# A log-sum-exp kernel with VectorE's instruction stream aligned to a block of 128

## The chip, the cores and the metric

The kernel runs on one core of a Trainium2 chip. A core has five engines with an instruction stream each: TensorE (PE in the profile), VectorE (DVE), ScalarE (ACT), GpSimd (POOL) and SyncE (SP). Here SyncE issues all the transfers, which sixteen DMA engines carry out. The metric is device time in microseconds, the median of several runs. The profile shows one execution; its span runs from the kernel's first instruction to its last.

## The reference

For each row of `x`, 32 x 512 rows of 1024 numbers in fp32, the logarithm of the sum of exponentials is computed, with the row's maximum taken out for safety.

```python
def reference(x):                      # x: 32 x 512 x 1024, standard normal
    max_x = np.max(x, axis=-1, keepdims=True)
    return (max_x.squeeze(-1) + np.log(np.sum(np.exp(x - max_x), axis=-1))).astype(np.float32)
```

## The kernel before

The 16,384 rows are spread over 128 partitions, 128 rows for each: 112 in one part, and the last 16 from another region of the input. The kernel sums the exponentials without the maximum, and checks afterwards that all sums are finite and of sane size. Only if they aren't does a fallback block repeat the work with the maximum (`with nc.If(all_fine < 1)`); on this data it is jumped over.

The rows come in through 18 loads of falling size (`LOADS`, from 16 rows for each partition to three quarters of a row) into a buffer `ring` that holds 48 rows for each partition. SyncE issues them (L130). The first load is moved ahead of the opening barrier. The next two wait for nothing but that barrier; from the fourth on, SyncE waits until the rows that lay in that part of the ring have been summed.

ScalarE takes the exponential of each load in place (L209). The sums are shared out by the letters in `LOADS`: for `R` VectorE reduces whole rows (L220); for `G` GpSimd first adds the two halves of each row (L215) and VectorE reduces the result (L146); for `T`, at the end, VectorE adds halves and accumulates in one instruction (L154). The very last quarters of a row are accumulated by ScalarE itself (L204). ScalarE then takes logarithms, and SyncE stores the results in two parts (L241 and, last of all, L251).

The order of the work on each engine is the order of the calls in the program: there is no scheduler. Waits on counted semaphores are written out by the small class `Counted`.

The closing part matters here. VectorE checks the sums (L161, L165), TensorE adds up the findings over the partitions (L171, L172, L255), and VectorE turns the number into a flag `fine` (L259). ScalarE and VectorE each load the flag into a register (L262) and branch (L311). On good sums both jump over their part of the fallback, which on VectorE is eleven instructions. Behind the jump each of the two signals SyncE (the signal of VectorE is L312, that of ScalarE is also shown under L311). SyncE waits for both signals, clears the semaphores (L315) and then waits for the last store (L317), with which the kernel ends.

The opening part is a barrier over all five engines, in three rounds (L355 and L59). VectorE's body, its first reduction, comes behind it.

Of the kernel before, what the change touches and what calls it, by code (L numbers as in the profile page):

```python
# [49 lines left out]
def kernel(  # L50
# [5 lines left out]
    nc = tc.nc  # L56
# [59 lines left out]
    stored = nc.alloc_semaphore("stored")  # L116

    nc.scalar.preload_act_table_set("natural_log_exp_and_others")  # L118
    pool.did(nc.gpsimd.memset(ones, 1.0))  # L119
    constants = pool.did(nc.gpsimd.memset(far, 100 * HIGH))  # L120

# [249 lines left out]
```

## Time and profile before

| What | us |
|---|---|
| median of 3 runs (162.53 to 162.91) | 162.78 |
| the profiled execution's own time | 162.55 |
| its span | 161.2 |
| VectorE busy | 119.1 |
| ScalarE busy | 115.1 |
| GpSimd busy | 32.4 |
| data read and written | 67.18 MB, 417 GB/s over the span |

A row of a line's view gives the engine, the operation, how often it ran, the shortest, middle and longest duration in nanoseconds, and the first and the last start in microseconds. An engine's name with a small q (DVEq, ACTq, SPq) stands for its sequencer: branches, semaphore steps and DMA issues, which don't count as busy. A row of the waits reads: who waited, for whom, microseconds in total, how often, the longest. The DMA view lists the packets by queue: their number, megabytes, and the time that they took as a share of sixteen engines over the window asked for. Times are counted from the start of the span, and a window may begin before it or end behind it.

### The profile page before, as it was taken

Reading aid. Unit: us, or ns where it says so; the run is one execution under the profiler, and the core shown is the slowest. Engines: PE = TensorE matmul, PEld = TensorE weight load, DVE = VectorE, ACT = ScalarE, POOL = GpSimd, SP = SyncE. Lnnn points to the kernel's source line nnn. Section 1 sums busy time; section 2 is a strip of 40 time slices with the busy share of each in tenths; the row PEclk is TensorE's granted clock in tenths of the full one; section 3 lists DMA queues with packets and bytes.
Section 4 is the critical chain, followed back from the end, with each engine's and each line's share of the span. In section 5 each row is a group of like instructions: output and inputs, shape, how many; then the busy total and the mean of one; then the engine's idle time right before and its main releaser. Section 6 shows DMA issues by size and latency. Waiting matters only on the chain.

```text
span 161.2 us, 183 instructions
## 1 busy us (share of the span) xinstructions
PE 0.5 (0%) x10; PEld 0.3 (0%) x10; DVE 119.1 (74%) x48; ACT 115.1 (71%) x32; POOL 32.4 (20%) x15
## 2 busy tenths in 40 slices
PE   0000000000000000000000000000000000000000
PEld 0000000000000000000000000000000000000000
DVE  0000000019999499995999999999999999999995
ACT  3000059980799609994199928996997999799995
POOL 0000000000000000000008800007950806727600
DMA  7996996996996996997999989898998999999990
GB/s 276 504 520 276 504 520 276 504 520 293 488 520 293 488 520 293 488 520 325 429 469 469 469 376 424 377 483 385 454 454 384 419 439 411 409 429 414 424 407 12
DMA packets 2880, 67.18 MB, mean 417 GB/s; under 512 B 576, under 2 KB 576, under 8 KB 1344
## 3 DMA queue, kind: packets, MB, share of 16 engines
q1 hardware_dynamic: 2880, 67.18, 97.2%
HBM read 67.11 MB, written 0.07 MB: 417 GB/s over the span
## 4 chain that ended last, share of the span: by engine, by line
DVE 53%; DMA 30%; ACT 12%; POOL 4%; PE 0%; issue 0%
DVE sumexp L220 38%; DMA ring<-in_x_dram 30%; ACT ring L209 12%; DVE sumexp L146 10%; POOL ring L215 4%; DVE ring L154 4%; DVE clamped L161 1%; DVE total L165 0%; PE count L171 0%; DVE fine L259 0%; PE count L255 0%; PE count L172 0%
## 5 line engine op out<-in xcount | busy, mean ns | idle before, releaser
L209 ACT ACTIVATE ring<-ring 128x16384 f32<-128x16384 f32 (+22 forms) x26 | 112.4, 4371 | 42.7 <-DMA ring<-in_x_dram 42.6
L220 DVE TENSOR_REDUCE sumexp<-ring 128x16 f32<-128x16384 f32 (+6 forms) x10 | 96.1, 9639 | 40.0 <-ACT ring L209 40.0
L215 POOL TENSOR_TENSOR ring<-ring 128x1024 f32<-128x1024 f32 (+5 forms) x9 | 32.1, 3573 | 118.3 <-ACT ring L209 118.3
L146 DVE TENSOR_REDUCE sumexp<-ring 128x2 f32<-128x1024 f32 (+5 forms) x9 | 16.1, 1802 | 0.4 <-POOL ring L215 0.4
L154 DVE SCALAR_TENSOR_TENSOR ring<-ring 128x512 f32<-128x512 f32 (+1 forms) x11 | 6.5, 642 | 0.0
L118 ACT ACT_TABLE_LOAD x1 | 1.3, 1283 | 1.4 <-PEq L59 1.4
L161 DVE SCALAR_TENSOR_TENSOR clamped<-sumexp 128x114 f32<-128x114 f32 (+1 forms) x2 | 0.9, 472 | 0.1
L204 ACT ACTIVATE ring<-ring 128x768 f32<-128x768 f32 x1 | 0.8, 843 | 0.1
L171 PE MATMUL count<-far,bad 128*1 128x1 f32 x4 | 0.4, 163 | 159.1 <-DVE total L165 159.1
L154 DVE DVE_READ_ACCUMULATOR ring<-ring 128x1 f32 x11 | 0.8, 76 | 0.0
L171 PEld LDWEIGHTS count<-far,bad 128*1 128x1 f32 x4 | 0.2, 80 | 159.2 <-POOL ring L215 151.1
L259 DVE TENSOR_SCALAR fine<-count 1x1 int32<-1x1 f32 x1 | 0.1, 146 | 0.4 <-PE count L255 0.4
L165 DVE TENSOR_REDUCE total<-sumexp 128x1 f32<-128x114 f32 (+1 forms) x2 | 0.4, 210 | 0.0
L172 PE MATMUL count<-total,ones 128*1 128x1 f32 x4 | 0.4, 163 | 0.0
L245 ACT ACTIVATE res<-sumexp 128x15 f32<-128x15 f32 x1 | 0.2, 215 | 0.1
L119 POOL MEMSET ones<- 128x1 f32 x1 | 0.1, 98 | 1.0 <-POOLq L59 1.0
L195 ACT ACTIVATE res<-sumexp 128x112 f32<-128x112 f32 x1 | 0.3, 280 | 0.0
L247 ACT ACTIVATE res<-sumexp 128x1 f32<-128x1 f32 x1 | 0.3, 278 | 0.0
L172 PEld LDWEIGHTS count<-total,ones 128*1 128x1 f32 x4 | 0.2, 81 | 0.0
L255 PE MATMUL count<-sumexp,ones 128*1 128x1 f32 x2 | 0.2, 163 | 0.0
L204 ACT ACTIVATION_READ_ACCUMULATOR ring<-ring 128x1 f32 x1 | 0.2, 187 | 0.0
L161 DVE DVE_READ_ACCUMULATOR clamped<-sumexp 128x1 f32 x2 | 0.2, 79 | 0.0
(6 smaller groups left out, 0.6 us busy)
## 6 DMA issues: line engine op xcount, KB each, us to landing
ring<-in_x_dram SPq DMA_DIRECT2D x1, 7376.0 KB, 24.9
ring<-in_x_dram SPq DMA_DIRECT2D x1, 5936.0 KB, 19.6
ring<-in_x_dram SPq DMA_DIRECT2D x1, 4768.0 KB, 16.4
ring<-in_x_dram SPq DMA_DIRECT2D x1, 3520.0 KB, 15.2
ring<-in_x_dram SPq DMA_DIRECT2D x1, 2976.0 KB, 21.9
ring<-in_x_dram SPq DMA_DIRECT2D x1, 1792.0 KB, 27.6
ring<-in_x_dram SPq DMA_DIRECT2D x1, 1520.0 KB, 25.2
ring<-in_x_dram SPq DMA_DIRECT2D x1, 1360.0 KB, 19.5
```

The costliest lines, as they stand in the source:

```text
L118: nc.scalar.preload_act_table_set("natural_log_exp_and_others")
L146: at = dve.did(nc.vector.reduce_sum(out=sumexp[:, c0 : c0 + s], in_=half, axis=AX.X))
L154: return dve.did(nc.vector.scalar_tensor_tensor(out=lo, in0=lo, scalar=1.0, in1=v[:, h : 2 * h], op0=ALU.mult, op1=ALU.add, accum_out=sume ...
L161: dve.did(nc.vector.scalar_tensor_tensor(out=clamped[:, c0:c1], in0=sumexp[:, c0:c1], scalar=LOW, in1=sumexp[:, c0:c1], op0=ALU.max, op1=A ...
L165: at = dve.did(nc.vector.reduce_sum(out=total[:, k : k + 1], in_=sumexp[:, c0:c1], axis=AX.X))
L171: pe.did(nc.tensor.matmul(count, lhsT=bad[:, k : k + 1], rhs=far, start=k == 0, stop=False))
L172: pe.did(nc.tensor.matmul(count, lhsT=ones, rhs=total[:, k : k + 1], start=False, stop=False))
L195: ln_early = act.did(nc.scalar.activation(out=res[:, 0:W], in_=sumexp[:, 0:W], func=AF.Ln))
L204: last = act.did(nc.scalar.activation(out=v, in_=v, func=AF.Exp, accum_out=sumexp[:, NC : NC + 1]))
L209: at = act.did(nc.scalar.activation(out=v, in_=v, func=AF.Exp))
L215: folded.append((c, p, s, pool.did(nc.gpsimd.tensor_tensor(out=rows[:, :, 0:H], in0=rows[:, :, 0:H], in1=rows[:, :, H:d], op=ALU.add,))))
L220: users.append((p, p + s * d, dve, dve.did(nc.vector.reduce_sum(out=sumexp[:, c : c + s], in_=rows, axis=AX.X))))
```

## The change

One line is added ahead of the kernel's first work instructions:

```diff
     nc.scalar.preload_act_table_set("natural_log_exp_and_others")
+    nc.vector.addr_align(128)
     pool.did(nc.gpsimd.memset(ones, 1.0))
     constants = pool.did(nc.gpsimd.memset(far, 100 * HIGH))
```

It is a directive in VectorE's stream. [...] The directive asks that the instruction that follows it on VectorE be placed at a multiple of 128 instructions; the space up to there is filled with instructions that do nothing, up to 127 of them. On VectorE it stands behind the last round of the opening barrier and ahead of the first reduction (L220). No work instruction, wait or transfer is added, removed or put into another order on any engine, and the streams of the other four engines stay as they were. All lines behind it have a number higher by one in the changed kernel.

## The prediction

> **What bounds the kernel.** I read the page first, then the chain of work that ended last, then the waits, and last the closing instructions line by line. The page's first part:
>
> ```profile
> span 161.2 us, 183 instructions
> PE 0.5 (0%) x10; PEld 0.3 (0%) x10; DVE 119.1 (74%) x48; ACT 115.1 (71%) x32; POOL 32.4 (20%) x15
> ```
>
> VectorE (DVE) has the longest list of work instructions, 48, and is busy for 74% of the span. The chain, in order of time (start, length, what), shows where that matters:
>
> ```profile
> 0.00 21.80 DMA ring<-in_x_dram
> ...
> 52.96 26.86 DMA ring<-in_x_dram
> ...
> 79.85 5.33 ACT ring L209
> ...
> 85.25 6.72 POOL ring L215
> ...
> 92.00 3.35 DVE sumexp L146
> 95.35 20.39 DVE sumexp L220 x2
> ...
> 159.71 0.15 DVE fine L259
> ```
>
> Up to 79.8 us the transfers set the time. From 92.00 on the chain is VectorE almost without a break, until the last small result `fine` at 159.86. The waits say when VectorE starts at all, and who closes the program:
>
> ```profile
> DVE sumexp L220 <- ACT ring L209: 40.0, 3, 35.7
> ...
> SPq L315 <- DVEq L312: 1.2, 1, 1.2
> ```
>
> VectorE's first reduction waits until 35.7 us. At the end the queue of SyncE (SP) waits for VectorE's closing signal, L312. This change touches only where instructions lie, so what follows `fine` is the place to look. The rows of lines L262, L311, L312, L315 and L317, each from the view of that line (duration, then start):
>
> ```profile
> L262 DVEq TENSOR_LOAD <-fine x1: 544/544/544, 159.9 to 159.9; - x1
> L311 ACTq COMPARE_BRANCH  x1: 45/45/45, 160.4 to 160.4; - x1
> L311 DVEq COMPARE_BRANCH  x1: 67/67/67, 160.5 to 160.5; - x1
> L311 ACTq EVENT_SEMAPHORE  x1: 17/17/17, 160.5 to 160.5; - x1
> L312 DVEq EVENT_SEMAPHORE  x1: 21/21/21, 161.0 to 161.0; - x1
> L315 SPq EVENT_SEMAPHORE_RANGE_CLEAR  x1: 71/71/71, 161.1 to 161.1; - x1
> L317 SPq EVENT_SEMAPHORE  x1: 17/17/17, 161.2 to 161.2; - x1
> ```
>
> The printed starts are coarse, so I asked the same views for windows of 0.01 us. ScalarE's (ACT's) branch is in progress in 160.42 to 160.43 and not in the next one, and its signal starts in 160.54 to 160.55: it needs 0.11 us from branch to signal. VectorE's branch ends in 160.54 to 160.55, and its signal starts only in 161.03 to 161.04: 0.49 us for the same step, a taken jump over the fallback block. Nothing in the profile is awaited there. SyncE's clear (L315) starts in 161.07 to 161.08, and L317 in 161.19 to 161.20, 0.12 us later; the span ends with it.
>
> **The change, part by part.**
>
> *The padding.* The directive stands behind the opening barrier (L59) and ahead of VectorE's first reduction. To reach a multiple of 128 takes at most 127 filler instructions on VectorE. The nearest rows for one filler are VectorE's four opening barrier steps:
>
> ```profile
> L59 DVEq DRAIN  x2: 10/10/10, 0.8 to 1.2; - x2
> L59 DVEq EVENT_SEMAPHORE  x2: 21/21/21, 1.1 to 1.4; - x2
> ```
>
> One lasts at least 0.01 us, so the least is 127 x 0.01 = 1.3 us. Four of them, waits included, fill 0.8 to 1.4 us, 0.15 each, so the most is 127 x 0.15 = 19 us. Both ends lie in the idle time from 1.4 to 35.7, 34.3 us. I take zero. Without that cover every microsecond of filler would lengthen the chain by one. Nothing else queues behind the filler: VectorE owes nobody anything before its first reduction ends, and SyncE's loads two and three do not wait for it.
>
> *The instruction blocks.* The trace has a queue for instruction fetches. Its answers for three windows, in this order: the microsecond from -9 to -8, the whole kernel up to 161.6, and 161.63 to 161.64:
>
> ```profile
> q14 instruction: 4, 0.03, 8.6%
> ...
> q1 hardware_dynamic: 2880, 67.18, 97.0%
> ...
> GB/s 0 0 0 0 0 0 0 0 0 0 0 0 0 0 0 0 0 0 0 0 0 0 0 0 0 0 0 0 32768 0 0 0 0 0 0 0 0 0 0 0
> q14 instruction: 1, 0.01, 332.5%
> ```
>
> Four blocks are fetched before the kernel starts. None is fetched while it runs: the second window has only the data queue. One more starts at 161.637 (the 29th fortieth of that window), behind the end of the span. A fortieth of 0.01 us at 32768 GB/s is 8192 bytes, and the first window's 0.03 MB for four agrees: a fetch is 8 KB. Alone, one takes 0.086 x 16 engines x 1 us / 4 = 0.34 us; the late one takes 3.325 x 16 x 0.01 = 0.53 us.
>
> So exactly one engine comes to a new block in this run, right about the end. VectorE has the longest stream, and it is the engine with the odd 0.49 us at its branch. I read the two together: VectorE's block boundary lies between its branch and the target, and the jump over it costs the excess. This is an inference; the trace doesn't name the engine that the fetch serves. With the body at the start of a block, the 48 work instructions, the loads of `fine`, the branch and the eleven fallback instructions behind it fit into 128, and branch and target share a block.
>
> *What it saves.* VectorE's own factor over ScalarE on the branch is 67/45 = 1.5, so without a boundary I expect 0.11 x 1.5 = 0.17 us for its exit, and the signal 0.49 - 0.17 = 0.32 us earlier, at 160.71. SyncE's clear would follow at 160.76 and L317 could run from 160.88. But L317 waits for the last store:
>
> ```profile
> 159.50 0.34 SPq L251 DMA_DIRECT2D out_dram<-res  x1
> ...
> DMA to landing us min/median/max: 1.4/1.4/1.4
> ```
>
> It lands at 159.50 + 1.4 = 160.9. With about 0.03 to 0.04 for the release (161.04 to 161.075 in the step from signal to clear), L317 starts at 160.94 in place of 161.19. The store is what is late next, and 0.25 us is what remains of 0.32. If the exit falls only to 0.35, the saving is 0.49 - 0.35 = 0.14, not yet limited by the store; if the store lands 0.07 earlier, it is 0.32. If the gap is simply VectorE's way to branch, it is zero.
>
> [...]
>
> *What it moves.* If entering a block sets off the fetch of the following one, the fetch now at 161.637 goes to the first microseconds, into the loads:
>
> ```profile
> 0.00:20.00 20.00, 0.00 (x0) 0.00 (x0) 0.00 (x0) 1.28 (x1) 0.34 (x6) 1.00 1.00 419
> ```
>
> The last two columns are the DMA engines' busy share, 1.00, and 419 GB/s: no room is left there. One 8 KB packet holds one of sixteen engines for 0.34 us. Shared by all it would be 0.02 us; if just that engine brings the last part of the load that lands at 79.8, the chain is late by the whole 0.34; if it isn't the last, by nothing. I take 0.02, which rounds away, since a load waits for one engine in sixteen, and keep 0.34 for the range. A fetch that VectorE has to wait for at the start is covered like the filler: even queued behind the whole first load it is there by 21.8 us, ahead of 35.7.
>
> **The sum.** The profiled execution took 162.55 us, its span 161.2 and 1.35 around it. Padding 0, exit -0.25, fetch +0.02 and so nothing: -0.25, a span of 160.95 and 162.30 for that execution. The median of the runs shown is 162.78, 0.23 above it, so I forecast 162.78 - 0.25 = 162.53 us, 0.15% less. About 0.2%, 0.33 us, is what a measurement of this kernel can tell from no change: the three runs shown spread over 0.38.
>
> **The rivals.**
>
> *The exit keeps its 0.49 us* because this is how VectorE leaves a branch, or because the late fetch belongs to another engine. [...] Against it: ScalarE's 0.11, and VectorE's branch itself is only 1.5 times as long. Time 162.78.
>
> *The fetch collides with the loads: slower.* Place: one DMA engine in the first 79.8 us. It decides when that engine is the last of the sixteen in the fourth load, and the exit gains nothing. Time 162.78 + 0.34 = 163.12. For it: the DMA share of 1.00. Against it: it must be the wrong engine, and the exit's saving, if it comes, pays for 0.25 of it, which leaves 162.87, inside 0.2%.
>
> *More than the exit is freed.* The late fetch, 161.64 to 162.17, lies inside the 1.35 us around the span. If VectorE's closing work waits for it, the alignment takes up to 0.53 more: 162.53 - 0.53 = 162.00, or, with half of it hidden, 162.27. For it: the fetch ends only 0.38 before the profiled execution's 162.55, if that time starts with the span. [...]
>
> **How the numbers follow.** The forecast, with the exit shorter by 0.14 to 0.32, gets 0.55; the unchanged exit 0.15; the collision 0.17; more than the exit 0.13. The forecast's saving ends just short of 0.33, and a median of few runs may fall 0.1 lower, so 0.17 of its 0.55 goes to faster and 0.38 to same. Faster: 0.17 + 0.13 = 0.30. Same: 0.38 + 0.15 = 0.53. Slower: 0.17. The range goes from 162.10, between the two ends of the third rival, to 163.10, just short of the full collision. The forecast's own range is 162.35 to 162.75.
>
> **What would show it.** Right: VectorE's signal within 0.2 us of its branch's end; L317 starting on the store's landing, near 160.9; no instruction fetch behind the span, and one in the first twenty microseconds; VectorE's first reduction still at 35.7; the fourth load landing at 79.8. Wrong: the exit still 0.49, or a fetch still at 161.6 (then it wasn't VectorE's, or the boundary isn't what costs); a first reduction later than 35.7 (the cover fails); a fourth load 0.1 or more later (the collision); or a span shorter by 0.25 with a time that doesn't follow it.

## The result

The changed kernel takes 162.96 us in the median (14 runs, 162.84 to 163.20), the kernel before 162.64 (14 runs, 162.47 to 162.97): a ratio of 1.0019, 95% interval 1.0013 to 1.0026. It is 0.3 us slower, clearly outside its own uncertainty, though just inside the 0.2% that the prediction took as the limit. The forecast was 0.25 us faster. The profiled execution took 163.01 us with a span of 161.7, against 162.55 and 161.2.

The page of the changed kernel, its first part and the DMA queues:

```profile
span 161.7 us, 240 instructions
PE 0.5 (0%) x10; PEld 0.4 (0%) x10; DVE 119.1 (74%) x48; ACT 115.0 (71%) x32; POOL 32.4 (20%) x15
...
q1 hardware_dynamic: 2880, 67.18, 97.0%
q14 instruction: 1, 0.01, 0.0%
```

The work is the same. The 57 instructions more (240 in place of 183) are the fillers, and an instruction fetch is now inside the span. Its chain of work, in order of time:

```profile
0.00 22.50 DMA ring<-in_x_dram
...
36.41 17.23 DVE sumexp L221
53.65 0.02 issue
53.66 26.90 DMA ring<-in_x_dram
...
80.58 5.33 ACT ring L210
...
92.74 3.35 DVE sumexp L147
...
160.44 0.15 DVE fine L260
```

The first load lands at 22.50 in place of 21.80. Everything behind it keeps that distance: VectorE's first reduction 36.41 (35.71), the fourth load 80.56 (79.83), VectorE's unbroken stretch from 92.74 (92.00), `fine` at 160.44 (159.71), 0.73 late. The loss is in the first load already. The rows by line:

```profile
L119 DVEq NOP  x57: 18/18/18, 1.5 to 4.1; - x57
L312 DVEq COMPARE_BRANCH  x1: 72/72/72, 161.2 to 161.2; - x1
L313 DVEq EVENT_SEMAPHORE  x1: 21/21/21, 161.4 to 161.4; - x1
L316 SPq EVENT_SEMAPHORE_RANGE_CLEAR  x1: 78/78/78, 161.5 to 161.5; - x1
L318 SPq EVENT_SEMAPHORE  x1: 17/17/17, 161.7 to 161.7; - x1
```

In windows of 0.01 us, VectorE's branch ends in 161.27 to 161.28 and its signal starts in 161.40 to 161.41: the exit fell from 0.49 us to 0.14. L318 starts in 161.65 to 161.66, so from the start of `fine` to L318 it is 1.21 us, against 161.19 - 159.71 = 1.48 before: 0.27 saved, on a chain that reaches this point 0.73 late. That makes 0.46, and the span is 161.7 against 161.2.

The fetch, asked for in the window 9.10 to 9.11 (a fortieth is 0.25 ns; the packet starts in the 21st, at 9.105):

```profile
GB/s 0 0 0 0 0 0 0 0 0 0 0 0 0 0 0 0 0 0 0 0 32768 0 0 0 0 0 0 0 0 0 0 0 0 0 0 0 0 0 0 0
q14 instruction: 1, 0.01, 193.1%
```

Its packet takes 1.931 x 16 x 0.01 = 0.31 us. Behind the span there is none any more: the window from 161.7 to 164 holds no packet at all.

### The profile page after: what moved, and what is told of

It is laid out like the page before. It is cut to its first block, busy times and chain, and to the rows that moved or that the text cites. A ratio compares the mean times of both kernels' runs of the same rounds, so it can differ in the third digit from the quotient of the medians.

```text
span 161.7 us, 240 instructions
## 1 busy us (share of the span) xinstructions
PE 0.5 (0%) x10; PEld 0.4 (0%) x10; DVE 119.1 (74%) x48; ACT 115.0 (71%) x32; POOL 32.4 (20%) x15
## 4 chain that ended last, share of the span: by engine, by line
DVE 52%; DMA 31%; ACT 12%; POOL 4%; PE 0%; issue 0%
DVE sumexp L221 38%; DMA ring<-in_x_dram 31%; ACT ring L210 12%; DVE sumexp L147 10%; POOL ring L216 4%; DVE ring L155 4%; DVE clamped L162 1%; DVE total L166 0%; PE count L172 0%; DVE fine L260 0%; PE count L256 0%; PE count L173 0%
```

## The experiments

All are the kernel before with the edit shown, next to `nc.vector.addr_align(128)`'s place in the changed kernel unless the edit says otherwise. Since the changed kernel has 57 fillers, the body of the kernel before starts at place 128 - 57 = 71 of its block. The theory after the result, from the two traces: entering a block sets off a fetch (at 9.105 in place of 161.637); a fetch among the loads makes them late (the first by 0.70); and an exit whose branch and target lie in one block is 0.35 us shorter (0.14 in place of 0.49). The traces give a fetch's size, 8 KB (32768 GB/s over 0.25 ns), and not what it brings: that it is a further block is the author's supposition.

**The fetch without the exit's saving (align_no_exit).**

```diff
+    nc.vector.addr_align(128)
+    nc.vector.addr_align(128, offset=71)
```

> The directive as in the changed kernel, and behind it a second one to place 71, so VectorE comes to a new block ahead of its body (57 fillers), and then 71 more fillers put the body back to the place in the block that it has in the kernel before. This takes the exit's saving out and leaves the fetch. Theory: fetch at 9.1 us, first load at 22.5 and fourth at 80.5 as in the changed kernel, exit 0.49, and a time 0.25 us above the changed kernel: some 0.55 to 0.7 over the kernel before, ratio 1.0035 to 1.0045. Rival (the exit's saving is worth nothing, since the store's landing or the closing sequence takes it): as the changed kernel, ratio 1.002 to 1.0025.

163.19 us against 162.60: 1.0038 (1.0024 to 1.0051), 0.6 slower. Its chain, its fillers and its closing rows:

```profile
0.00 22.39 DMA ring<-in_x_dram
...
160.34 0.14 DVE fine L261
```

```profile
L119 DVEq NOP  x57: 18/18/18, 1.5 to 4.1; - x57
L120 DVEq NOP  x71: 18/18/18, 4.6 to 7.9; - x71
L313 DVEq COMPARE_BRANCH  x1: 72/72/72, 161.1 to 161.1; - x1
L314 DVEq EVENT_SEMAPHORE  x1: 21/21/21, 161.7 to 161.7; - x1
```

The late load is there (22.39), and the exit is back at 0.50 us, since VectorE's body has its old place in a block again. A fetch behind the branch is back with it, at 162.26. The time is 0.23 us above the changed kernel's median, and by the two ratios 0.19%, 0.3 us. So the exit's saving is real and worth what the prediction said, and it is hidden under a fetch that costs twice as much. The theory's numbers held; the rival's 1.0020 to 1.0025 did not.

The fillers also show the boundary by itself. Fillers follow each other every 0.047 us (57 from 1.5 to 4.1), but between the 57th, which starts in 4.10 to 4.15, and the next, in 4.55 to 4.60, lie 0.46. So in this run VectorE's sequencer stands still for about 0.4 us (0.46 less 0.047) at the boundary, without a jump too.

**Twice the fetch (two_fetches), and an inadvertent repeat (two_blocks).**

```diff
+    nc.vector.addr_align(128)
+    nc.vector.addr_align(128, offset=1)
+    nc.vector.addr_align(128)
```

> Three directives (to 0, to 1, to 0 again): 57 + 1 + 127 fillers, two boundaries ahead of the body. In the run two_blocks the idle instruction between had been dropped, and the trace had 57 fillers. Theory: a second fetch in the first 30 us over the same DMA engine, the first or second load late by another 0.7 (23.2 in all), time 0.8 to 1.1 over the kernel before. Rival (a fetch costs the loads only once, for example as a slot that stays reserved): as the changed kernel.

163.90 us against 162.60: 1.0082 (1.0068 to 1.0096), 1.3 slower. Its DMA view for 9 to 10 and for 14 to 15 us, and its chain:

```profile
q14 instruction: 1, 0.01, 1.9%
...
q14 instruction: 1, 0.01, 2.0%
```

```profile
0.00 23.38 DMA ring<-in_x_dram
...
161.33 0.15 DVE fine L262
```

Two fetches, and the first load 1.58 later than before, 0.88 more than with one. Here each of the two fetches had its cost.

two_blocks was meant as this experiment, with an idle instruction between two directives:

```diff
+    nc.vector.addr_align(128)
+    nc.vector.nop(nofuse=True)
+    nc.vector.addr_align(128)
```

> The directive stands twice, with one idle instruction between, so VectorE comes to two new blocks ahead of its body: 57 + 1 + 127 = 185 fillers, some 9 us of 0.047, still covered by the wait to 35.7. Theory: two fetches in the first 20 us, and if both go over the same DMA engine the first load is late by up to 1.4 us, and the time 1.0 to 1.2 us over the kernel before; if a fetch costs the load only once, as the changed kernel. Exit 0.14. Rival (fillers): late by 185/57 of 0.7, 2.3 us.

The idle instruction does not appear in the trace, which has 57 fillers and one fetch, so this is the changed kernel over again. It gave 1.0029 (1.0018 to 1.0041) and a first load at 22.53, which tells only that the result repeats.

**Where the fetch falls (off127, off108, off84).**

```diff
+    nc.vector.addr_align(128, offset=127)
```

> The body begins at the last place of a block, 127: 56 fillers, one fewer than the changed kernel, but the boundary lies behind the first reduction, so the fetch starts only when VectorE goes on to the second, after 36 us. Theory: exit 0.14; the first load lands at 21.8 as before, and the load in flight at the fetch (the second, third or fourth) is the first that comes late, by about 0.7; time as the changed kernel, 0.3 us over the kernel before. Rival (fillers): the first load is late by 0.7 already, as in the changed kernel. Second rival (the first loads are late or not from one execution to the next): no tie between the fetch and the first late load.

163.04 us, 1.0027 (1.0016 to 1.0037), the exit 0.14. The first load was late at once, 22.50, as the rival had it. But the fetch was early too: it starts in the first ten microseconds, at 9.096, though VectorE's only instruction ahead of the boundary is the first reduction, which waits until 36.4. So this run does not tell fillers from fetch. It shows one fetch, at 9.096, set off while VectorE still waited on the near side.

```diff
+    nc.vector.addr_align(128, offset=108)
```

> The body begins at place 108 of a block in place of 0. The changed kernel has 57 fillers, so the body of the kernel before begins at place 71; here there are 37 fillers and the boundary lies behind the 20th work instruction, which starts at about 151 us. Theory (the lateness of the loads comes from the instruction fetch, the short exit from branch and target in one block): VectorE's exit 0.14 us as in the changed kernel; first load landed at 21.8 and fourth at 79.8 as before; one fetch at 151 to 157; time 0.25 us under the kernel before (ratio 0.9985). Rival (the fillers themselves, or the directive, make the loads late): first load later by 37/57 of 0.7, 0.45 us, and time 0.2 us over the kernel before.

163.15 us, 1.0037 (1.0024 to 1.0049). The fetch came in 96 to 97, not at 151. Its DMA view for that microsecond, its chain and VectorE's timeline:

```profile
q14 instruction: 1, 0.01, 1.9%
```

```profile
1.44 39.72 DMA ring<-in_x_dram
...
72.32 25.67 DMA ring<-in_x_dram
97.99 0.02 issue
```

```profile
116.34 2.82 DVE L147 TENSOR_REDUCE sumexp<-ring 128x5 f32<-128x2560 f32 x1 [0.56 <-POOL ring L216]
```

This is the clearest of the three. 37 fillers ran at the start, and the first loads came as before: the second landed at 41.16, where ScalarE had taken that load up at 41.15 in the kernel before. The fifth, in flight at the fetch, landed at 97.99, where ScalarE had taken it up at 97.25 before; from then on the chain is late, and VectorE, without a gap there before, waits 0.56 at 115.8. That excludes the fillers, and ties the lateness to the fetch. The gain expected did not come, because the fetch was not where I had put it.

```diff
+    nc.vector.addr_align(128, offset=84)
```

> The body begins at place 84: 13 fillers, the boundary behind the 44th work instruction, at about 159 us, still ahead of VectorE's branch. Theory: exit 0.14, first load at 21.8, one fetch behind 160; time 0.25 us under the kernel before, unless the fetch meets the last store, which would cost up to 0.3. Rival (fillers): first load later by 13/57 of 0.7, 0.16 us, time about 0.1 under the kernel before.

162.60 us, 1.0002 (0.9994 to 1.0011). The exit is 0.14, the first load lands at 21.84, but the fetch came in 155 to 156 and met the last two loads. ScalarE's and VectorE's timelines:

```profile
157.63 0.84 ACT L210 ACTIVATE ring<-ring 128x768 f32<-128x768 f32 x1 [0.74 <-DMA ring<-in_x_dram]
```

```profile
158.50 0.69 DVE L155 SCALAR_TENSOR_TENSOR ring<-ring 128x512 f32<-128x512 f32 x1 [0.27 <-ACT ring L210]
```

ScalarE waits 0.74 us for a load, which it did not before, and 0.27 of it reaches VectorE: about what the exit saves.

**The fetches of other engines (gpsimd_align, scalar_align).**

```diff
+    nc.gpsimd.addr_align(128)
```

> VectorE is left as before; the directive stands on GpSimd, ahead of its two small fills, whose results are needed only at 151 us. Theory: GpSimd comes to a new block, one fetch goes out in the first 15 us, and one DMA engine is late by about 0.7: first load landed at 22.5, VectorE's exit still 0.49, time 0.5 to 0.7 us over the kernel before (ratio 1.003 to 1.004), more than the changed kernel because nothing is saved at the exit. If the fetches of GpSimd run over another DMA engine, the load may be late by less, 0.1 to 0.7. Rival (what makes the loads late is something of VectorE): loads at 21.8, ratio 1.000.

162.94 us against 162.56: 1.0024 (1.0015 to 1.0033). GpSimd's 54 fillers ran from 1.4 to 3.5, and a fetch went out at 8.95.

```diff
+    nc.scalar.addr_align(128)
```

> VectorE is left as before; the directive stands on ScalarE, behind the request for its table and ahead of its first exponential, which waits for the first load until 21.8. Theory: as for GpSimd, one fetch in the first 15 us, first load late by up to 0.7, VectorE's exit 0.49, ScalarE's exit 0.11 as before, time 0.3 to 0.7 us over the kernel before. Rival (VectorE alone): ratio 1.000.

162.95 us, 1.0025 (1.0015 to 1.0034), 56 fillers on ScalarE, a fetch at 9.02. The chains of gpsimd_align and of scalar_align:

```profile
0.00 22.01 DMA ring<-in_x_dram
...
53.17 26.91 DMA ring<-in_x_dram
```

```profile
0.00 22.12 DMA ring<-in_x_dram
...
53.28 26.89 DMA ring<-in_x_dram
```

VectorE is untouched in both, its exit 0.49, and both are 0.4 us slower in the medians (0.5 to 0.7 was expected of gpsimd_align): the rival that something of VectorE makes the loads late is out. The first loads landed at 22.01 and 22.12, only 0.2 and 0.3 behind the kernel before, and the runs without an early fetch spread from 21.80 to 21.96. With VectorE's early fetch alone it was 22.39 to 22.53. Both profiled executions are also among the quickest of their kernels (162.80 and 162.89), so one trace shows less than the medians.

Both also keep the fetch behind VectorE's branch, at 161.90 and 161.98. No run whose VectorE branch and target share a block has one there, and every run in which the boundary lies between them has it (the kernel before, off76 below, align_no_exit): it is VectorE's, as the prediction inferred.

**The exit, and a version without the collision (off76, late_align, off80, off82).**

```diff
+    nc.vector.addr_align(128, offset=76)
```

> The body begins at place 76: 5 fillers, and the boundary behind the 52nd place of the body, which should still lie between VectorE's branch and its target. Theory: the exit stays at 0.49, in spite of a directive in the stream; the fetch starts a little earlier than the 161.6 of the kernel before, at 158 to 161, behind the last load or with it; time as before or up to 0.3 over it (ratio 1.000 to 1.002). Rival (any alignment shortens the exit, or the exit isn't a matter of the boundary): 0.14 here too.

162.59 us, 1.0000 (0.9991 to 1.0010). Five fillers, the boundary still between branch and target:

```profile
L312 DVEq COMPARE_BRANCH  x1: 67/67/67, 160.6 to 160.6; - x1
L313 DVEq EVENT_SEMAPHORE  x1: 21/21/21, 161.1 to 161.1; - x1
```

The exit is 0.47. With the directive at place 84 it was 0.14: it is the boundary between branch and target that costs, not the absence of a directive. The fetch came at 162.0, behind the branch as before, and not at 158 to 161.

```diff
+    nc.vector.addr_align(128)
     dve.wait(pe, at)
     at = dve.did(nc.vector.tensor_scalar(out=fine, in0=count, scalar1=HIGH, ...
```

> The directive moves from the start of VectorE's body to just ahead of `fine`, the last work instruction, where VectorE waits 0.38 us for TensorE. Counted from place 71, `fine` stands at place 118, so some 10 fillers of 0.047 us, 0.47 in all, mostly under that wait. Theory: branch and target share a block, so the exit is 0.14 and not 0.49; nothing changes ahead of it, so the loads land as before (21.8, 79.8, last one 158.0), and the fetch starts behind the last load. Time 0.25 us under the kernel before, ratio 0.9985, limited by the store's landing; if the fetch meets the last store (159.5 to 160.9), nothing or up to 0.3 less gain. Rival (the exit's saving is not worth anything in the time, because the closing sequence waits for something else): ratio 1.000 with an exit of 0.14.

162.60 us, 0.9999 (0.9990 to 1.0008). Loads as before (21.90), exit 0.14, but nothing gained. VectorE's fillers and timeline:

```profile
L258 DVEq NOP  x10: 18/18/18, 159.2 to 159.6; - x10
```

```profile
160.12 0.15 DVE L260 TENSOR_SCALAR fine<-count 1x1 int32<-1x1 f32 x1 [0.68 <-PE count L255]
```

`fine` starts after 0.68 of idle time in place of 0.38. The fillers end at 159.6, so the rest is a stop at the boundary, as between the fillers above. It moved ahead of `fine`, cost 0.30 us there and took the saving. Neither the theory nor the rival had this.

```diff
+    nc.vector.addr_align(128, offset=80)
```

> 9 fillers, the boundary behind the 48th place of the body, ahead of the load of `fine`. Theory: exit 0.14. If the fetch starts at 157 to 158, it meets only the tail of the last load, and the time is 0.1 to 0.25 us under the kernel before; if VectorE stops at the boundary itself as in late_align, where `fine` came 0.30 late, the load of `fine` comes some 0.3 late and the time is as before.

162.48 us against 162.60: 0.9995 (0.9986 to 1.0004). Exit 0.14, fetch at 157.3, no stop ahead of `fine` or of its load. Its closing rows:

```profile
L313 DVEq EVENT_SEMAPHORE  x1: 21/21/21, 160.8 to 160.8; - x1
L316 SPq EVENT_SEMAPHORE_RANGE_CLEAR  x1: 91/91/91, 160.9 to 160.9; - x1
L318 SPq EVENT_SEMAPHORE  x1: 17/17/17, 161.0 to 161.0; - x1
```

VectorE signals at 160.8 in place of 161.0, and the last store, issued at 159.62, lands at 161.0, so L318 waits for the store, as the prediction had it. The median is the lowest of all, but the interval holds 1; whether it beats the kernel before is not settled.

```diff
+    nc.vector.addr_align(128, offset=82)
```

> 11 fillers, the boundary behind the 46th place, ahead of the last small sum (L165 of the kernel before), which has work of VectorE ahead of it to hide a stop. Theory: exit 0.14; fetch between off84's 155.5 and off80's; time 0 to 0.2 us under the kernel before. A stop of 0.3 at the boundary would show as idle time ahead of that sum.

162.65 us, 1.0003 (0.9994 to 1.0012): exit 0.14, no stop at the boundary, fetch at 155.8, among the last loads as in off84. Two places more than off80, and what off80 may gain is gone.

## Why the prediction was wrong

*Padding, 0 us: right.* 57 fillers ended at 4.1, inside the 34.3 us of cover. One took 0.047, between the 0.01 and the 0.15 of the bounds. VectorE's first reduction is late because its load is late, and off108 shows 37 fillers with the first loads on time.

*"Four blocks are fetched before the kernel starts": four in the window shown.* The trace has two more fetches between -15 and -10 us. Nothing in the sum rests on their number.

*Whose fetch, and where the boundary is: right.* gpsimd_align and scalar_align keep the late fetch, and off76 against off84 puts the boundary between branch and target.

*Exit, -0.25: right.* 0.49 fell to 0.14 (0.17 was expected), L318 came on the store's landing, and 0.27 was saved from `fine` on. align_no_exit returns 0.23 of it in the medians.

*"I take 0.02, which rounds away", the fetch among the loads: this is the step that failed.* It was foreseen that the fetch would move into the first microseconds, and that the DMA engines had no room (a busy share of 1.00). The size was wrong twice. The upper end, 0.34, was the mean length of the four fetches' packets between -9 and -8 of the kernel before, where the view shows no other packet; in the trace of the changed kernel the packet is no longer (0.31), and yet the first load is 0.70 late and the fourth 0.73. The data packet that starts as the fetch's ends takes 0.53 longer; the two make 0.84 (last section), a loss of one DMA engine if they share it, which was not shown. And the value inside the bounds was taken as if sixteen engines could share the work, though in the changed kernel fourteen of the first load's sixteen landing steps had come by 21.80 and the load landed with the last, at 22.50 (last section). Nothing between the first load and the fourth took the delay up. align_no_exit measures the term alone: 0.6 us in the medians. With 0.6 in place of 0.02 the sum is -0.25 + 0.6 = +0.35, and 0.32 was measured.

*The rivals.* "The fetch collides with the loads" was the right mechanism, with 0.17. Its point of decision was wrong: it asked for an exit that gains nothing as well, and gave 162.87, inside 0.2%, for a collision with the exit's saving. What happened is this mixed case, only with a larger price. "The exit keeps its 0.49" and "more than the exit is freed" are both refuted: the exit fell, and from the span to the whole time it is 1.3 us in both profiled executions (163.01 - 161.7 and 162.55 - 161.2).

## What to carry to other kernels

In this kernel the DMA engines' busy share is 1.00 in the first 20 us, and one instruction fetch of 8 KB there went with a first load 0.70 us late. Moving VectorE's block boundary moved the fetch, from 161.6 to 9.1, so look where the fetch goes, not only at the stall that it leaves: here a stall of 0.35 us at the end was traded for 0.6 us at the start. And price a small transfer that meets such a stretch by what the next landing loses (0.70 here), not by the length of its own packet (0.31).

## What was unexpected

One fetch of 8 KB by VectorE cost 0.6 to 0.9 us of the chain in these runs (0.59 in the first load of align_no_exit, 0.70 in that of the changed kernel, 0.88 for the second of two_fetches) while its packet shows 0.31 (0.32 for that second one). The packet of data that follows is longer too. The DMA view of the changed kernel for 9.37 to 9.38, where an ordinary data packet starts, and for 9.405 to 9.415, where the fetch ends (9.105 + 0.31):

```profile
q1 hardware_dynamic: 1, 0.07, 1512.5%
...
q1 hardware_dynamic: 1, 0.07, 1842.5%
```

The ordinary packet of 64 KB takes 15.125 x 16 x 0.01 = 2.42 us, the one behind the fetch 2.95. In the first two microseconds of the changed kernel many data packets take longer, 2.6 to 3.7; after them, in each run with a fetch in the first load, the packets of this size that start as a fetch ends are the only ones over 2.6. The fetch and what the packet behind it takes longer make 0.31 + 0.53 = 0.84 us. For the second fetch of two_fetches it is 0.32 + 0.66 = 0.98, for GpSimd's 0.31 + 0.21 = 0.52 and for ScalarE's 0.31 + 0.24 = 0.55. That the two packets share a DMA engine, which would lose these sums, is the author's supposition.

The trace also has sixteen steps of a load's semaphore. For the first load they come from 21.25 to 21.80 in the kernel before. In two_fetches fifteen have come by 21.84 and the last comes at 23.38; in off127 it is 21.75 and 22.50. In the changed kernel two are late: fourteen by 21.80, then 22.22 and 22.50. So the sixteen do not share the delay in these runs. If one step is one engine, which was not shown, the load is late by what the engine with the fetch loses, less the lead that it had over the last one. The smaller delays with GpSimd's and ScalarE's fetches (0.21 and 0.32) would fit that. Why a data packet takes longer behind a fetch, and more behind VectorE's (0.53 and 0.66) than behind theirs (0.21 and 0.24), is not shown, and the trace doesn't name the DMA engine of a packet.

What sets a fetch off is also open. In the kernel before, off76 and late_align it starts 1.1 to 1.4 us behind the crossing, and each of these shows a stop of 0.3 to 0.35 us there. Where fillers cross it among the first loads, it starts 4 to 5.5 us behind. In off80, off82 and off84 it starts before the boundary is reached (in off80 at 157.3, with `fine`, ahead of the boundary, at 159.83), and no stop is seen. In off108 VectorE was at its fourth and fifth work instruction, 16 places ahead of the boundary, some 4 us before the fetch. A look-ahead of those 16 places that hides the stop when it has time to run, a guess of the author's, would fit these, but the late fetches of the kernel before and of off76 don't follow from it, and it wasn't tried by itself.
